# Gates and branch projections with the activations as the stationary operand

## The chip, the cores and the metric

The kernel runs on one core of a Trainium2 chip. The metric is the device time of one execution in microseconds; lower is better. Every matmul is preceded by the load of its stationary operand (PEld in the profile); the other operand moves through the array column by column.

## What is computed

A decoder trunk of two layers on 256 tokens of width 1024, in float32. The attention heads are 12 of dilated windows (branch a), 6 of block attention (b) and 6 of stick-breaking attention (c). The part around the change:

```python
h = rmsnorm(x, norm_mix)
proj = h @ w_in                                   # q, k, v and three gates of width 1024
gates = jax.nn.sigmoid(proj[..., 3 * MIX_WIDTH:]).reshape(B, S, 3, D)
y_a = flat(o_a) @ w_out_a                         # 256 -> 1024
y_b = flat(o_b) @ w_out_b                         # 384 -> 1024
y_c = flat(o_c) @ w_out_c                         # 384 -> 1024
merged = gates[:, :, 0] * y_a + gates[:, :, 1] * y_b + gates[:, :, 2] * y_c
x = x + merged @ w_o
h = rmsnorm(x, norm_mlp)
x = x + jnp.square(jax.nn.relu(h @ w_up)) @ w_down
```

## The kernel before

The activations lie transposed: channels on the 128 partitions in 8 tiles (KT), the 256 tokens (S) along the free dimension. For precision each float32 operand is split into a high and a low part of a shorter format (hi, lo), and each product is three matmuls: hi by lo of the weight, hi by hi, lo by hi.

**Weights** come in 280 pieces of 128 x 1024 (140 a layer), in the order in which they are used. load (L91) fetches a piece by DMA into one of 4 raw buffers; split_one (L106) makes its parts, wh by ScalarE (L115) and wl by VectorE (L116), in 6 buffers each, three pieces ahead of use and at raised priority. proj (L188) multiplies one weight tile, stationary, with the activations of all 256 tokens, moving: 3 matmuls of 256 columns for each of the 8 channel tiles, 24 in all.

**Stages of a layer**: values (v_chunk, L232, with activations stationary and 512 weight columns moving); queries and keys (qk_pair, L261) and gates (gate_tile, L453), between which units of the attention (att_softmax, att_c) are put as MIX_ORDER (L50) and UNIT_RATE (L44) say; the sigmoids; the **branch stage** (L489 to L503); the output projection (L506 to L513); then the MLP (up_pair, L539; down, L554, and in the last layer down_nat, L581, which has activations stationary).

gate_tile(d) makes the three gates of one channel tile, 3 x 24 matmuls into two PSUM banks, which ScalarE copies to G[d] (L459). After the last exponential of the layer, ScalarE loads the table of the sigmoid, applies it to G[0] to G[7] (L483) and, in the first layer, loads the table of exp and ln back (L486). The branch stage goes by channel tile d: into one s tile of two PSUM banks come the three branch projections (2, 3 and 3 channel tiles of oT), VectorE multiplies all 768 columns by the gates (L499), adds the three parts (L500, L501), and ScalarE and VectorE split the sum into mg (L502, L503). The output projection then takes mg as its moving operand, and VectorE adds the result to the residual xres (L511), from which norm_split (L152) makes the operand of the MLP.

**PSUM** has 8 banks: two of tag mm, two of tag t, and two s tiles of two banks each. **The order** on each engine is made by a scheduler ahead of time from the order in the program, the priorities and its own estimates; the engines then run their lists strictly in that order and wait on semaphores.

Of the kernel before, what the change touches and what calls it, by code (L numbers as in the profile page):

```python
# [15 lines left out]
P = 128  # L16
# [24 lines left out]
NORM_ACT = False  # L41
TAIL = 4
SKEW = 2
UNIT_RATE = {"v": 2, "qk": 1, "g": 2}  # L44
SWAP = [8, 9, 10, 11, 12, 13, 14, 15, 0, 1, 2, 3, 4, 5, 6, 7] + list(range(16, 32))

# [12 lines left out]
def trunk(ctx: ExitStack, tc: tile.TileContext, w, x, norms, gfin, consts, out):  # L59
# [18 lines left out]
    def mm_bank():  # L78
        return PS("mm", [P, 512], 2)
# [67 lines left out]
    negtri, negones = tri[:, 0], tri[:, 1]  # L147

    def hilo_slot():
        return T("hl", [P, 2, KT, S], 2, F32R)  # L150

    def norm_split(hl, nrm, d):  # L152

        g = cst["norms"][:, nrm, d:d + 1]
        act.activation(hl[:, 0, d], xres[:, d], AF.Copy, scale=g)
        dve.scalar_tensor_tensor(hl[:, 1, d], xres[:, d], g, hl[:, 0, d].bitcast(F32),
                                 op0=ALU.mult, op1=ALU.subtract)

    def sumsq(d, acc):
# [28 lines left out]
    def proj(dst, n, hl, nk=KT, first=True, last=True, koff=0, woff=0):  # L188

        hi, lo = split(n)  # L190
        for k in range(nk):
            c = (woff + k) * P
            a = (first and k == 0)
            z = (last and k == nk - 1)
            pe.matmul(dst, lo[:, c:c + P], hl[:, 0, koff + k], start=a, stop=False, skip_group_check=True)  # L195
            pe.matmul(dst, hi[:, c:c + P], hl[:, 0, koff + k], start=False, stop=False, skip_group_check=True)  # L196
            pe.matmul(dst, hi[:, c:c + P], hl[:, 1, koff + k], start=False, stop=z, skip_group_check=True)  # L197

    acc = T("acc", [P, S], 1)
    hl = hilo_slot()  # L200
# [9 lines left out]
    for layer in range(DEPTH):  # L210
# [9 lines left out]
        def normalized():  # L220

            for d in range(KT):
                t = T("sq", [P, S], 3)
                g = cst["norms"][:, 2 * layer, d:d + 1]
                dve.scalar_tensor_tensor(t, xres[:, d], g, R, op0=ALU.mult, op1=ALU.mult)
                act.activation(xh[:, 0, d], t, AF.Copy)
                dve.tensor_tensor(xh[:, 1, d], t, xh[:, 0, d].bitcast(F32), op=ALU.subtract)  # L227


        V = {}  # L230
# [1 line left out]
        def v_chunk(c, n):  # L232
            if c == 0:
                pv = [mm_bank(), mm_bank()]
            else:
                sb = s_bank()
                pv = [sb[:, 0], sb[:, 1]]
            for q in range(4):
                hi, lo = split(n + q)
                for kk in range(2):  # L240
                    k = 2 * q + kk
                    wsl = slice(kk * 512, kk * 512 + 512)
                    for t in range(2):
                        tsl = slice(t * P, t * P + P)
                        pe.matmul(pv[t], xs[:, 0, k, tsl], lo[:, wsl], start=k == 0, stop=False)  # L245
                        pe.matmul(pv[t], xs[:, 0, k, tsl], hi[:, wsl], start=False, stop=False)
                        pe.matmul(pv[t], xs[:, 1, k, tsl], hi[:, wsl], start=False, stop=k == KT - 1)  # L247
# [46 lines left out]
            dve.tensor_tensor(oF[j * DH:(j + 1) * DH], po[0:DH, 0:S], tmp, op=ALU.add)  # L294

        def o_split(oF, kt):
            last_exp[0] = act.activation(oT[:, 0, kt], oF, AF.Copy)
            dve.tensor_tensor(oT[:, 1, kt], oF, oT[:, 0, kt].bitcast(F32), op=ALU.subtract)

        def pv_mm(po, head, kt, ph, pl, first, last):  # L300

# [158 lines left out]

        units = []

# [4 lines left out]

        n = base
        for kind, i in MIX_ORDER:
            {"v": v_chunk, "qk": qk_pair, "g": gate_tile}[kind](i, n)  # L470
            n += MIX_LEN[kind]
            group, u = ATT_AFTER.get((kind, i), (None, 0))
            if group == "a":
                att_softmax(QK_A[u], u, units)
            elif group == "b":
                att_softmax([QK_B[u]], 2 + u, units)
            elif group == "c":
                att_c(u, units)
            run_units(UNIT_RATE[kind])
        run_units(len(units))  # L480
        with tc.issue_after(last_exp[0].ins):
            for d in range(KT):
                s = act.activation(G[d], G[d], AF.Sigmoid)  # L483
# [6 lines left out]
        for d in range(KT):  # L490
# [12 lines left out]
            dve.tensor_tensor(mg[:, 1, d], m3[:, 0], mg[:, 0, d].bitcast(F32), op=ALU.subtract)  # L503


        acc = T("acc", [P, S], 1)  # L506
        hl = hilo_slot()
        for d in range(KT):
            p = mm_bank() if d % 2 else t_bank()
            proj(p[:, 0:S], base + 68 + d, mg)  # L510
# [28 lines left out]
        def up_pair(i):  # L539
            p = mm_bank()  # L540
            proj(p[:, 0:S], npc["u", 2 * i], hl)
            proj(p[:, S:2 * S], npc["u", 2 * i + 1], hl)
            s1 = T("wk", [P, 512], WK)
            act.activation(s1, p, AF.Relu)
            u = T("wk", [P, 512], WK)
            act.activation(u, s1, AF.Square)
            uh = T("ga", [P, 2, S], KT, F32R)
            ul = T("ga", [P, 2, S], KT, F32R)
# [131 lines left out]
def weight_pieces(w_in, w_out_a, w_out_b, w_out_c, w_o, w_up, w_down):  # L680
    out = np.empty((DEPTH * PIECES, P, 1024), np.float32)

    def cols(w, f):
        return w[:, f * P:(f + 1) * P].reshape(KT, P, P).transpose(1, 0, 2).reshape(P, 1024)

    for layer in range(DEPTH):
        n = layer * PIECES
        wi = w_in[layer]
# [6 lines left out]
        for kind, i in MIX_ORDER:  # L695
            if kind == "v":
                out[n:n + 4] = vcols(i)
            elif kind == "qk":
                out[n] = cols(wi[:, :MIX], i)
                out[n + 1] = cols(wi[:, MIX:2 * MIX], i)  # L700
            else:
                for b in range(3):
                    out[n + b] = cols(gw[:, b * D:(b + 1) * D], i)
            n += MIX_LEN[kind]
        wy = np.concatenate([w_out_a[layer], w_out_b[layer], w_out_c[layer]], axis=0)
        for d in range(KT):
            out[n] = cols(wy, d)
            n += 1
        for d in range(KT):
            out[n] = cols(w_o[layer], d)  # L710
            n += 1
# [37 lines left out]
```

## Time and profile before

| | us |
|---|---|
| median of 3 runs (lowest, highest) | 893.87 (893.34, 893.88) |
| the profiled execution | 893.46 |
| its span in the profile | 891.4 |
| busy: TensorE matmul / weight load | 878.8 / 837.8 |
| busy: VectorE / ScalarE / GpSimd | 602.4 / 491.7 / 52.4 |

The difference of 2.06 us between the profiled execution and its span lies outside the profile's first and last instruction. A matmul's record is longer than its step, because matmuls overlap in the array: what counts is the distance of the starts.

### The profile page before, as it was taken

To read this page: it belongs to the slowest core of one execution; us is meant where nothing else is said; L and a number is where in the kernel's file an instruction comes from. 1 tells how busy PE (TensorE), PEld (TensorE's weight loads), DVE (VectorE), ACT (ScalarE), POOL (GpSimd) and SP (SyncE) were. 2 spreads that over 40 slices of the span, in tenths; PEclk is the share of its full clock that TensorE was granted. 3 is DMA by queue.
4 is the path that set the end of the run, shared out by engine and by line. 5 is a ranking of instruction groups with operands and counts; after the bars stand their busy time and mean duration, and the time that the engine had idled before them with its cause. 6 is when DMAs were issued, how large, how long until landed. Compare 5 with 4: busy or idle time off the path is not lost.

```text
span 891.4 us, 16382 instructions
## 1 busy us (share of the span) xinstructions
PE 878.8 (99%) x6672; PEld 837.8 (94%) x6672; DVE 602.4 (68%) x899; ACT 491.7 (55%) x724; POOL 52.4 (6%) x72
## 2 busy tenths in 40 slices
PE   8999999999999999999999999999999999999996
PEld 6899999999999999999988999999999999999995
DVE  7887787774985455555588878777667865555554
ACT  5655566668465444444466555666573654444442
POOL 6000000000020000000020100000000400000000
PEclk9999999999999999999999999999999999999999
DMA  8764444544656656555556544444555666666641
GB/s 302 232 197 144 140 129 138 158 147 131 199 167 192 193 183 189 182 177 185 165 176 203 167 148 136 141 125 139 164 165 168 194 197 192 186 186 189 187 137 47
DMA packets 43562, 151.47 MB, mean 170 GB/s; under 512 B 4960, under 2 KB 6368, under 8 KB 43488
## 3 DMA queue, kind: packets, MB, share of 16 engines
q1 hardware_dynamic: 43056, 149.90, 54.6%
q8 instruction: 52, 0.85, 0.4%
q10 hardware_dynamic: 432, 0.54, 0.2%
q14 instruction: 22, 0.18, 0.1%
HBM read 149.37 MB, written 1.05 MB: 169 GB/s over the span
## 4 chain that ended last, share of the span: by engine, by line
PE 94%; DVE 3%; issue 1%; DMA 1%; ACT 0%; SPq 0%; POOLq 0%; DVEq 0%; ACTq 0%
PE mm L195 18%; PE mm L197 18%; PE mm L196 18%; PE s L561 3%; PE s L563 3%; PE s L562 3%; PE s L587 3%; PE s L588 3%; PE s L589 3%; PE s L280 2%; PE s L195 2%; PE s L197 2%; PE s L196 2%; PE s L245 2%; DVE wl L116 2%; PE s L247 2%
## 5 line engine op out<-in xcount | busy, mean ns | idle before, releaser
L116 DVE TENSOR_TENSOR wl<-raw,wh 128x1024 fp32r<-128x1024 f32 (+1 forms) x282 | 345.5, 1228 | 228.2 <-ACT wh L115 227.4
L115 ACT ACTIVATE wh<-raw 128x1024 fp32r<-128x1024 f32 (+1 forms) x282 | 295.2, 1051 | 296.4 <-PE mm L197 160.8
L195 PE MATMUL mm<-hl,wl 128*128 128x256 f32 x1344 | 383.2, 285 | 1.4 <-DVE xres L511 1.4
L196 PE MATMUL mm<-hl,wh 128*128 128x256 f32 x1344 | 381.5, 284 | 0.0
L197 PE MATMUL mm<-hl,wh 128*128 128x256 f32 x1344 | 380.1, 284 | 0.0
L195 PEld LDWEIGHTS mm<-hl,wl 128*128 128x128 f32 x1344 | 257.1, 191 | 5.8 <-DVE xres L511 1.8
L196 PEld LDWEIGHTS mm<-hl,wh 128*128 128x128 f32 x1344 | 257.1, 191 | 0.9
L197 PEld LDWEIGHTS mm<-hl,wh 128*128 128x128 f32 x1344 | 256.5, 191 | 0.7 <-DVE hl L227 0.2
L561 PE MATMUL s<-ga,wl 128*128 128x256 f32 x256 | 72.5, 284 | 0.0
L562 PE MATMUL s<-ga,wh 128*128 128x256 f32 x256 | 72.3, 283 | 0.0
L563 PE MATMUL s<-ga,wh 128*128 128x256 f32 x256 | 72.2, 283 | 0.0
L587 PE MATMUL s<-wl,ga 128*128 128x512 f32 x128 | 50.1, 391 | 0.0
L588 PE MATMUL s<-wh,ga 128*128 128x512 f32 x128 | 50.0, 391 | 0.0
L561 PEld LDWEIGHTS s<-ga,wl 128*128 128x128 f32 x256 | 49.1, 192 | 0.5 <-DVE sq L648 0.2
L589 PE MATMUL s<-wh,ga 128*128 128x512 f32 x128 | 49.5, 389 | 0.0
L562 PEld LDWEIGHTS s<-ga,wh 128*128 128x128 f32 x256 | 49.1, 192 | 0.1
L563 PEld LDWEIGHTS s<-ga,wh 128*128 128x128 f32 x256 | 49.0, 192 | 0.2 <-DVE ga L550 0.2
L166 POOL TENSOR_TENSOR acc<-acc,sq 128x256 f32<-128x256 f32 x21 | 20.8, 991 | 404.4 <-ACT sq L165 229.8
L195 PE MATMUL s<-hl,wl 128*128 128x256 f32 x128 | 36.4, 285 | 0.0
L197 PE MATMUL s<-hl,wh 128*128 128x256 f32 x128 | 36.3, 284 | 0.0
L196 PE MATMUL s<-hl,wh 128*128 128x256 f32 x128 | 36.2, 283 | 0.0
L587 PEld LDWEIGHTS s<-wl,ga 128*128 128x128 f32 x128 | 24.1, 188 | 5.0 <-DVE V L622 0.4
(139 smaller groups left out, 1143.4 us busy)
## 6 DMA issues: line engine op xcount, KB each, us to landing
raw<-in_w_dram SPq DMA_DIRECT2D x278, 512.0 KB, 4.0
raw<-in_w_dram SPq DMA_DIRECT2D x4, 256.0 KB, 4.7
xres<-in_x_dram SPq DMA_DIRECT2D x8, 128.0 KB, 5.1
wk<-in_gfin_dram SPq DMA_DIRECT2D x2, 256.0 KB, 4.0
out_dram<-V SPq DMA_DIRECT2D x2, 256.0 KB, 2.3
out_dram<-V ACTq DMA_DIRECT2D x2, 256.0 KB, 2.2
c_maskA<-in_maskA_dram SPq DMA_DIRECT2D x1, 384.0 KB, 5.4
c_rope<-in_rope_dram SPq DMA_DIRECT2D x1, 256.0 KB, 4.9
```

Source lines behind the costliest of these rows:

```text
L115: act.activation(hi[:, c:c + step], r[:, c:c + step], AF.Copy)
L116: dve.tensor_tensor(lo[:, c:c + step], r[:, c:c + step], hi[:, c:c + step].bitcast(F32), op=ALU.subtract)
L166: pool.tensor_tensor(acc, acc, sq, op=ALU.add)
L195: pe.matmul(dst, lo[:, c:c + P], hl[:, 0, koff + k], start=a, stop=False, skip_group_check=True)
L196: pe.matmul(dst, hi[:, c:c + P], hl[:, 0, koff + k], start=False, stop=False, skip_group_check=True)
L197: pe.matmul(dst, hi[:, c:c + P], hl[:, 1, koff + k], start=False, stop=z, skip_group_check=True)
L561: pe.matmul(dst, lo[:, c], uh[:, j % 2], start=a, stop=False, skip_group_check=True)
L562: pe.matmul(dst, hi[:, c], uh[:, j % 2], start=False, stop=False, skip_group_check=True)
L563: pe.matmul(dst, hi[:, c], ul[:, j % 2], start=False, stop=z, skip_group_check=True)
L587: pe.matmul(dst, uh[:, j % 2, k], lo[:, c], start=j == 0, stop=False)
L588: pe.matmul(dst, uh[:, j % 2, k], hi[:, c], start=False, stop=False)
L589: pe.matmul(dst, ul[:, j % 2, k], hi[:, c], start=False, stop=j == 2 * npairs - 1)
```

## The change

Gates and branch projections are computed with tokens on the partitions: the activations of 128 tokens are the stationary operand, and 512 weight columns move. gate_chunk (L455 of the changed kernel) makes 512 columns of one gate for both token halves t in the two mm banks, in two halves of the contraction, with a unit of attention between them; there are 6 chunks of 4 pieces a layer for 8 tiles of 3. The branch stage (L504 to L531) goes by column half h, branch br and token half t: an s tile has one bank for each t, VectorE multiplies it by the gate (L519, L522) and adds it to the sum m[t] (L523). As the output projection wants channels on partitions, TensorE transposes m[t] in four 128 x 128 blocks into a t bank (L527), and ScalarE and VectorE split from there into mg (L530, L531). The first two tiles of the output projection are computed in two halves of the contraction (L537 to L539). In the activation tiles hi and lo now lie next to each other for each channel tile (layout [P, KT, 2, S] for [P, 2, KT, S]). The gates lie in 6 buffers of 4 KB a partition for 8 of 3 KB; the up stage of the MLP puts uh and ul in one such buffer, six pairs for four. The core of the diff:

```diff
-             ("g", 5), ("g", 6), ("g", 7)]
-MIX_LEN = {"v": 4, "qk": 2, "g": 3}
+             ("g", 5)]
+MIX_LEN = {"v": 4, "qk": 2, "g": 4}
+BRANCH_K = [(0, 1), (2, 3, 4), (5, 6, 7)]
...
-        G = [T("ga", [P, 3, S], KT) for _ in range(KT)]
-
-        def gate_tile(d, n):
-            gf = G[d].rearrange("p a b -> p (a b)")
-            for b0, nb in ((0, 2), (2, 1)):
-                p = mm_bank()
-                for b in range(nb):
-                    proj(p[:, b * S:(b + 1) * S], n + b0 + b, xh)
-                act.activation(gf[:, b0 * S:(b0 + nb) * S], p[:, 0:nb * S], AF.Copy)
+        G = {}
+
+        def gate_chunk(i, n):
+
+            G[i] = T("ga", [P, 2, 512], GA_BUFS)
+            pg = [mm_bank(), mm_bank()]
+            for half in range(2):
+                for t in range(2):
+                    tsl = slice(t * P, t * P + P)
+                    for q in (2 * half, 2 * half + 1):
+                        hi, lo = split(n + q)
+                        for kk in range(2):
+                            k = 2 * q + kk
+                            wsl = slice(kk * 512, kk * 512 + 512)
+                            pe.matmul(pg[t], xh[:, k, 0, tsl], lo[:, wsl], start=k == 0, stop=False)
+                            pe.matmul(pg[t], xh[:, k, 0, tsl], hi[:, wsl], start=False, stop=False)
+                            pe.matmul(pg[t], xh[:, k, 1, tsl], hi[:, wsl], start=False, stop=k == KT - 1)
+                    if half == 1:
+                        act.activation(G[i][:, t], pg[t], AF.Copy)
+                if half == 0:
+                    run_units(1)
...
-        for d in range(KT):
-            n = base + 60 + d
-            st = s_bank()
-            sf = st.rearrange("p a b -> p (a b)")
-            proj(sf[:, 0:S], n, oT, nk=2, koff=0, woff=0)
-            proj(sf[:, S:2 * S], n, oT, nk=3, koff=2, woff=2)
-            proj(sf[:, 2 * S:3 * S], n, oT, nk=3, koff=5, woff=5)
-            m3 = T("wk", [P, 3, S], WK)
-            m3f = m3.rearrange("p a b -> p (a b)")
-            dve.tensor_tensor(m3f, sf[:, 0:3 * S], G[d].rearrange("p a b -> p (a b)"), op=ALU.mult)
-            dve.tensor_tensor(m3[:, 0], m3[:, 0], m3[:, 1], op=ALU.add)
-            dve.tensor_tensor(m3[:, 0], m3[:, 0], m3[:, 2], op=ALU.add)
-            act.activation(mg[:, 0, d], m3[:, 0], AF.Copy)
-            dve.tensor_tensor(mg[:, 1, d], m3[:, 0], mg[:, 0, d].bitcast(F32), op=ALU.subtract)
+        for h in range(2):
+            n = base + 60 + 4 * h
+            m = [T("wk", [P, 512], WK) for t in range(2)]
+            for br, ks in enumerate(BRANCH_K):
+                st = s_bank()
+                for t in range(2):
+                    tsl = slice(t * P, t * P + P)
+                    for k in ks:
+                        hi, lo = split(n + k // 2)
+                        wsl = slice(k % 2 * 512, k % 2 * 512 + 512)
+                        pe.matmul(st[:, t], oT[:, k, 0, tsl], lo[:, wsl], start=k == ks[0], stop=False)
+                        pe.matmul(st[:, t], oT[:, k, 0, tsl], hi[:, wsl], start=False, stop=False)
+                        pe.matmul(st[:, t], oT[:, k, 1, tsl], hi[:, wsl], start=False, stop=k == ks[-1])
+                    g = G[2 * br + h][:, t]
+                    if br == 0:
+                        dve.tensor_tensor(m[t], st[:, t], g, op=ALU.mult)
+                    else:
+                        y = T("wk", [P, 512], WK)
+                        dve.tensor_tensor(y, st[:, t], g, op=ALU.mult)
+                        dve.tensor_tensor(m[t], m[t], y, op=ALU.add)
+            for t in range(2):
+                tb = t_bank()
+                for d in range(4):
+                    pe.transpose(tb[:, d * P:(d + 1) * P], m[t][:, d * P:(d + 1) * P], ident)
+                t4 = tb.rearrange("p (a b) -> p a b", a=4)
+                mh, ml = (mg[:, 4 * h:4 * h + 4, x, t * P:(t + 1) * P] for x in range(2))
+                act.activation(mh, t4, AF.Copy)
+                dve.tensor_tensor(ml, t4, mh.bitcast(F32), op=ALU.subtract)
...
+        pw = [mm_bank(), mm_bank()]
+        for first in (True, False):
+            for d in range(2):
+                proj(pw[d][:, 0:S], base + 68 + d, mg, nk=4, first=first, last=not first, koff=0 if first else 4, woff=0 if first else 4)
```

**The order at three places** of the first layer, as the programs have it; in brackets stand the engines on whose semaphores an instruction waits. First TensorE in the branch stage before: s_465, s_470 and s_475 are the s tiles of three channel tiles, and 24 matmuls stand between one mark and the next.

```order
L195 MATMUL s_465_2668<-hl_23_169,wl_454_2561 128x256
L196 MATMUL s_465_2668<-hl_23_169,wh_453_2560 128x256
L197 MATMUL s_465_2668<-hl_23_169,wh_453_2560 128x256
...
L195 MATMUL s_470_2705<-hl_23_169,wl_458_2593 128x256 [waits DVE_49]
L196 MATMUL s_470_2705<-hl_23_169,wh_457_2592 128x256
L197 MATMUL s_470_2705<-hl_23_169,wh_457_2592 128x256
...
L195 MATMUL s_475_2742<-hl_23_169,wl_463_2635 128x256 [waits DVE_49]
```

The same place now: s_456 is the tile of branch a (6 matmuls for each token half), s_460 that of b, s_469 that of c (9 each), which takes the buffer of s_456; all of column half 0. Runs of matmuls between the marks are left out.

```order
L516 MATMUL s_456_2333<-wh_445_2263,hl_23_169 128x512
...
L514 MATMUL s_460_2354<-wl_452_2300,hl_23_169 128x512 [waits Activation_49]
...
L516 MATMUL s_460_2354<-wh_451_2299,hl_23_169 128x512 [waits DVE_49]
L514 MATMUL s_456_2333<-wl_446_2264,hl_23_169 128x512 [waits DVE_49]
L515 MATMUL s_456_2333<-wh_445_2263,hl_23_169 128x512
...
L514 MATMUL s_469_2391<-wl_452_2300,hl_23_169 128x512 [waits DVE_49]
L515 MATMUL s_469_2391<-wh_451_2299,hl_23_169 128x512
...
L514 MATMUL s_460_2354<-wl_449_2288,hl_23_169 128x512 [waits DVE_49]
```

The second token half of s_456 waits for VectorE after 9 other matmuls, and s_469 waits for VectorE directly behind it. Second, ScalarE at the sigmoids before; ga_24 to ga_31 are the gates of the eight channel tiles.

```order
L297 ACTIVATE hl_23_169<-oF_356_2002 128x256 [waits DVE_49]
L483 ACT_TABLE_LOAD
L483 ACTIVATE ga_24_170<-ga_24_170 128x768
...
L483 ACTIVATE ga_29_175<-ga_29_175 128x768 [waits Activation_49]
L483 ACTIVATE ga_30_176<-ga_30_176 128x768 [waits Activation_49]
...
L459 ACTIVATE ga_31_177<-mm_448_2527 128x512
...
L459 ACTIVATE ga_31_177<-mm_455_2589 128x256
...
L483 ACTIVATE ga_31_177<-ga_31_177 128x768 [waits Activation_49]
L486 ACT_TABLE_LOAD
```

The same place now.

```order
L299 ACTIVATE hl_23_169<-oF_376_1992 128x256 [waits DVE_49]
L497 ACT_TABLE_LOAD
L497 ACTIVATE ga_135_793<-ga_135_793 128x1024
L497 ACTIVATE ga_235_1316<-ga_235_1316 128x1024
L497 ACTIVATE ga_331_1783<-ga_331_1783 128x1024
L497 ACTIVATE ga_382_2009<-ga_382_2009 128x1024
L497 ACTIVATE ga_418_2151<-ga_418_2151 128x1024 [waits Activation_49]
L497 ACTIVATE ga_438_2246<-ga_438_2246 128x1024 [waits Activation_49]
L500 ACT_TABLE_LOAD
L117 ACTIVATE wh_471_2397<-raw_470_2395 128x1024 [waits DMAHW2_49,PE_49]
```

Before, gate evictions still followed on the first seven sigmoids; now all of them stand ahead of the sigmoids, and the next weight split stands behind the six sigmoids and the load of the table. Third, VectorE at the end of the branch stage now; wk_478 is the sum of column half 1 and token half 1, t_498 the transposes of token half 0. Before there were no transposes, and this place had only the products, sums and splits of the channel tiles.

```order
L118 TENSOR_TENSOR wl_509_2566<-raw_507_2563,wh_508_2565 128x1024 [waits DMAHW0_49,Activation_49]
L522 TENSOR_TENSOR wk_497_2524<-s_492_2496,ga_438_2246 128x512 [waits PE_49]
L118 TENSOR_TENSOR wl_514_2619<-raw_512_2616,wh_513_2618 128x1024 [waits DMAHW1_49,Activation_49]
L531 TENSOR_TENSOR hl_453_2330<-t_498_2527,hl_453_2330 128x4x128 [waits Activation_49]
L523 TENSOR_TENSOR wk_478_2437<-wk_478_2437,wk_497_2524 128x512 [waits DVE_49]
L531 TENSOR_TENSOR hl_453_2330<-t_499_2534,hl_453_2330 128x4x128 [waits Activation_49]
```

The last sum (L523) stands behind two weight splits and a subtraction, and the last group of transposes (t_499) needs it.

## Rows read from the trace of the kernel before

**Rows 1.** Part 1 of the page: busy us (share of the span) x instructions.

```profile
PE 878.8 (99%) x6672; PEld 837.8 (94%) x6672; DVE 602.4 (68%) x899; ACT 491.7 (55%) x724; POOL 52.4 (6%) x72
```

**Rows 2.** Part 4 of the page: the chain that ended last, by engine.

```profile
PE 94%; DVE 3%; issue 1%; DMA 1%; ACT 0%; SPq 0%; POOLq 0%; DVEq 0%; ACTq 0%
```

**Rows 3.** Timeline, TensorE, last gates of layer one: start, us, engine, line, operation.

```profile
207.76 0.28 PE L195 MATMUL mm<-hl,wl 128*128 128x256 f32 x1
...
216.28 0.28 PE L197 MATMUL mm<-hl,wh 128*128 128x256 f32 x1
```

**Rows 4.** Timeline, TensorE, down projection of the last layer, activations stationary.

```profile
741.68 0.39 PE L588 MATMUL s<-wh,ga 128*128 128x512 f32 x1
...
743.95 0.39 PE L589 MATMUL s<-wh,ga 128*128 128x512 f32 x1
```

**Rows 5.** Windows, branch stage: stretch, length, busy PE, PEld, DVE, ACT, POOL, clock, DMA.

```profile
229.00:246.00 17.00, 17.00 (x144) 17.00 (x143) 15.95 (x28) 6.91 (x11) 0.00 (x0) 1.00 0.58 162
```

**Rows 6.** Timeline, TensorE: a value matmul, three stalls, the last matmul.

```profile
207.06 0.22 PE L307 MATMUL t<-pl,V 128*64 128x128 f32 x1
...
224.08 0.28 PE L197 MATMUL s<-hl,wh 128*128 128x256 f32 x1
224.35 0.39 PE L195 MATMUL s<-hl,wl 128*128 128x256 f32 x1
...
250.25 0.28 PE L197 MATMUL mm<-hl,wh 128*128 128x256 f32 x1
250.69 0.39 PE L195 MATMUL t<-hl,wl 128*128 128x256 f32 x1 [0.16 <-DVE xres L511]
...
264.81 0.29 PE L196 MATMUL mm<-hl,wh 128*128 128x256 f32 x1
265.93 0.39 PE L195 MATMUL mm<-hl,wl 128*128 128x256 f32 x1 [0.84 <-DVE xres L511]
...
884.27 0.39 PE L589 MATMUL s<-wh,ga 128*128 128x512 f32 x1
```

**Rows 7.** Timeline, TensorE, four transposes inside a stream of matmuls.

```profile
711.13 0.60 PE L576 MATMUL t<-c_ident,xres 128*128 128x128 f32 x4
711.49 0.36 PE L197 MATMUL mm<-hl,wh 128*128 128x256 f32 x1
711.69 0.28 PE L195 MATMUL mm<-hl,wl 128*128 128x256 f32 x1
```

**Rows 8.** Groups by line and form: count, busy us, mean ns, idle before.

```profile
L116 DVE TENSOR_TENSOR wl<-raw,wh 128x1024 fp32r<-128x1024 f32 x278 | 341.5, 1231 | 222.5 <-ACT wh L115 221.7
L115 ACT ACTIVATE wh<-raw 128x1024 fp32r<-128x1024 f32 x278 | 292.7, 1057 | 292.1 <-PE mm L197 160.8 <-PE s L563 38.9 <-PE s L589 33.7
L272 DVE TENSOR_TENSOR qk<-qk,sh 128x512 f32<-128x512 f32 x18 | 12.4, 686 | 0.2
L483 ACT ACTIVATE ga<-ga 128x768 f32<-128x768 f32 x16 | 12.2, 832 | 0.0
L270 DVE TENSOR_TENSOR qk<-mm,c_rope 128x512 f32<-128x512 f32 x18 | 12.1, 672 | 0.0
L459 ACT ACTIVATE ga<-mm 128x512 f32<-128x512 f32 x16 | 9.4, 589 | 0.1
```

**Rows 9.** Timeline, ScalarE, around the sigmoids of the first layer.

```profile
209.64 0.42 ACT L297 ACTIVATE hl<-oF 128x256 fp32r<-128x256 f32 x1 [1.06 <-DVE oF L294]
210.08 1.28 ACT L483 ACT_TABLE_LOAD   x1
211.37 5.25 ACT L483 ACTIVATE ga<-ga 128x768 f32<-128x768 f32 x7
...
222.05 1.28 ACT L486 ACT_TABLE_LOAD   x1
```

**Rows 10.** Windows at the end of the trace, same columns as rows 5.

```profile
888.00:889.00 1.00, 0.00 (x0) 0.00 (x0) 0.00 (x0) 0.00 (x0) 0.00 (x0) 0.60 0.45 170
889.00:890.00 1.00, 0.00 (x0) 0.00 (x0) 0.00 (x0) 0.00 (x0) 0.00 (x0) 0.50 0.91 354
```

More of the change, by code (lines that the diff above doesn't have):

```diff
@@ L43 @@
 SKEW = 2
+GA_BUFS = 6
 UNIT_RATE = {"v": 2, "qk": 1, "g": 2}
@@ L149, in hilo_slot @@
     def hilo_slot():
-        return T("hl", [P, 2, KT, S], 2, F32R)
+        return T("hl", [P, KT, 2, S], 2, F32R)
     def norm_split(hl, nrm, d):
         g = cst["norms"][:, nrm, d:d + 1]
-        act.activation(hl[:, 0, d], xres[:, d], AF.Copy, scale=g)
-        dve.scalar_tensor_tensor(hl[:, 1, d], xres[:, d], g, hl[:, 0, d].bitcast(F32),
+        act.activation(hl[:, d, 0], xres[:, d], AF.Copy, scale=g)
+        dve.scalar_tensor_tensor(hl[:, d, 1], xres[:, d], g, hl[:, d, 0].bitcast(F32),
                                  op0=ALU.mult, op1=ALU.subtract)
@@ L194, in proj @@
             z = (last and k == nk - 1)
-            pe.matmul(dst, lo[:, c:c + P], hl[:, 0, koff + k], start=a, stop=False, skip_group_check=True)
-            pe.matmul(dst, hi[:, c:c + P], hl[:, 0, koff + k], start=False, stop=False, skip_group_check=True)
-            pe.matmul(dst, hi[:, c:c + P], hl[:, 1, koff + k], start=False, stop=z, skip_group_check=True)
+            pe.matmul(dst, lo[:, c:c + P], hl[:, koff + k, 0], start=a, stop=False, skip_group_check=True)
+            pe.matmul(dst, hi[:, c:c + P], hl[:, koff + k, 0], start=False, stop=False, skip_group_check=True)
+            pe.matmul(dst, hi[:, c:c + P], hl[:, koff + k, 1], start=False, stop=z, skip_group_check=True)
     acc = T("acc", [P, S], 1)
@@ L225, in normalized @@
                 dve.scalar_tensor_tensor(t, xres[:, d], g, R, op0=ALU.mult, op1=ALU.mult)
-                act.activation(xh[:, 0, d], t, AF.Copy)
-                dve.tensor_tensor(xh[:, 1, d], t, xh[:, 0, d].bitcast(F32), op=ALU.subtract)
+                act.activation(xh[:, d, 0], t, AF.Copy)
+                dve.tensor_tensor(xh[:, d, 1], t, xh[:, d, 0].bitcast(F32), op=ALU.subtract)
         V = {}
@@ L244, in v_chunk @@
                         tsl = slice(t * P, t * P + P)
-                        pe.matmul(pv[t], xs[:, 0, k, tsl], lo[:, wsl], start=k == 0, stop=False)
-                        pe.matmul(pv[t], xs[:, 0, k, tsl], hi[:, wsl], start=False, stop=False)
-                        pe.matmul(pv[t], xs[:, 1, k, tsl], hi[:, wsl], start=False, stop=k == KT - 1)
+                        pe.matmul(pv[t], xs[:, k, 0, tsl], lo[:, wsl], start=k == 0, stop=False)
+                        pe.matmul(pv[t], xs[:, k, 0, tsl], hi[:, wsl], start=False, stop=False)
+                        pe.matmul(pv[t], xs[:, k, 1, tsl], hi[:, wsl], start=False, stop=k == KT - 1)
             V[c] = T("V", [P, 2, 8, 2, DH], 3, F32R)
@@ L296, in o_split @@
         def o_split(oF, kt):
-            last_exp[0] = act.activation(oT[:, 0, kt], oF, AF.Copy)
-            dve.tensor_tensor(oT[:, 1, kt], oF, oT[:, 0, kt].bitcast(F32), op=ALU.subtract)
+            last_exp[0] = act.activation(oT[:, kt, 0], oF, AF.Copy)
+            dve.tensor_tensor(oT[:, kt, 1], oF, oT[:, kt, 0].bitcast(F32), op=ALU.subtract)
         def pv_mm(po, head, kt, ph, pl, first, last):
@@ L481, in trunk @@
         with tc.issue_after(last_exp[0].ins):
-            for d in range(KT):
-                s = act.activation(G[d], G[d], AF.Sigmoid)
+            for i in range(6):
+                s = act.activation(G[i], G[i], AF.Sigmoid)
         if layer < DEPTH - 1:
@@ L506, in trunk @@
         acc = T("acc", [P, S], 1)
         hl = hilo_slot()
+        pw = [mm_bank(), mm_bank()]
+        for first in (True, False):
+            for d in range(2):
+                proj(pw[d][:, 0:S], base + 68 + d, mg, nk=4, first=first, last=not first, koff=0 if first else 4, woff=0 if first else 4)
         for d in range(KT):
-            p = mm_bank() if d % 2 else t_bank()
-            proj(p[:, 0:S], base + 68 + d, mg)
+            if d < 2:
+                p = pw[d]
+            else:
+                p = mm_bank() if d % 2 else t_bank()
+                proj(p[:, 0:S], base + 68 + d, mg)
@@ L546, in up_pair @@
             act.activation(u, s1, AF.Square)
-            uh = T("ga", [P, 2, S], KT, F32R)
-            ul = T("ga", [P, 2, S], KT, F32R)
+            uu = T("ga", [P, 2, 2, S], GA_BUFS, F32R)
+            uh, ul = uu[:, 0], uu[:, 1]
             dve.tensor_copy(uh.rearrange("p a b -> p (a b)"), u)
@@ L684, in cols, with halves @@
         return w[:, f * P:(f + 1) * P].reshape(KT, P, P).transpose(1, 0, 2).reshape(P, 1024)
+    def halves(w):
+        return w.reshape(KT // 2, 2, P, 512).transpose(0, 2, 1, 3).reshape(4, P, 1024)
     for layer in range(DEPTH):
@@ L701, in weight_pieces @@
             else:
-                for b in range(3):
-                    out[n + b] = cols(gw[:, b * D:(b + 1) * D], i)
+                out[n:n + 4] = halves(gw[:, i * 512:(i + 1) * 512])
             n += MIX_LEN[kind]
         wy = np.concatenate([w_out_a[layer], w_out_b[layer], w_out_c[layer]], axis=0)
-        for d in range(KT):
-            out[n] = cols(wy, d)
-            n += 1
+        for h in range(2):
+            out[n:n + 4] = halves(wy[:, h * 512:(h + 1) * 512])
+            n += 4
         for d in range(KT):
```

3 lines of the change are left out of this document (1 added, 2 removed).

## The prediction

> **What bounds the kernel now.** I read the page's busy shares first: TensorE is busy for 99% of the span [rows 1]. As matmuls are pipelined, that proves little, so the chain of waits comes next: 94% of it is TensorE, 3% VectorE [rows 2]. The kernel is bound by the rate at which matmuls follow each other, and that is read from the start times in the timeline. Matmuls with 256 moving columns start 0.120 us apart, 72 of them without a gap from 207.76 to 216.28 [rows 3]. With 512 columns it is 0.227 us, ten steps from 741.68 to 743.95 [rows 4]. One wide matmul thus replaces two narrow ones and saves 0.240 - 0.227 = 0.013 us. VectorE is the second thing to watch: in the branch stage it is busy 15.95 of 17 us [rows 5] while TensorE does not wait for it. TensorE loses almost nothing there now: three stalls in each layer, of 0.15, 0.32 and 1.0 us beyond the step of 0.12 [rows 6].
>
> **The change, part by part.**
> *Gates.* Before, 8 tiles x 3 x 24 = 576 narrow matmuls per layer; now 6 chunks x 48 = 288 wide ones. *Branch projections.* 8 x 24 = 192 narrow ones become 2 x 8 x 2 x 3 = 96 wide ones. Together 384 per layer, 768 in all, x 0.013 = **-10.0 us**, all on the bounding engine.
>
> The Trainium skill (TensorE: Matmul & The Clock Gate, "Back-to-back issue gap") speaks against this gain: N/2.4 + 2.5 ns gives 109 ns and 216 ns for the two widths, a saving of 2.6 ns, so 2.0 us in all and a time of 914. The rows have 120 and 227 ns in long unbroken stretches, and I go by them.
>
> *Transposes.* 4 groups of 4 per layer are new. Four such transposes stand inside a stream of narrow matmuls: from 711.13 to 711.49, and the step after them is 0.08 too long, so 0.44 us a group [rows 7]. 8 groups: **+3.5 us**.
>
> *The branch stage's waits.* This is where I expect the loss. Before, one s tile took three projections (24 matmuls, 2.9 us) and two such tiles alternated, so VectorE had 2.9 us to empty one. Now a tile holds two token halves, and its second half waits for VectorE to have multiplied the first; the next use of the tile waits for the multiply of the second. The order shows these waits on TensorE, with little or nothing between a half and the matmul that waits for its reading. Prices, all from [rows 8] unless named: a multiply out of PSUM 0.67, an add or a subtraction 0.69, a weight split 1.06 on ScalarE and then 1.23 on VectorE (an operation that is followed at once counts 0.07 less), the copy out of PSUM 0.59; a wide matmul's result is there 0.39 after its start [rows 4], 0.16 after the next could start. I add about 0.04 for each hand-over. First layer:
> 1. The first multiply needs the first sigmoid, which follows the last head's split. Before, that split ended at 210.06 [rows 9], 3.0 us after the last value matmul at 207.06 [rows 6]; the table load took 1.28 [rows 9]. A sigmoid of 1024 columns is estimated at 0.83 + 0.24 = 1.07 (768 columns take 0.83, a 512-column eviction 0.59). So 3.0 + 1.28 + 1.07 + 0.67 + 0.1 = 6.1 us until TensorE may write the second half. It has 14 wide matmuls before that, 3.2 us: **2.9**. Before, gate matmuls filled this time: the table load began at 210.08, the gates ended at 216.28 [rows 3, 9].
> 2. The tile's next use directly behind its second half: 0.16 + 0.67 + 0.1 = **0.9**.
> 3. The second tile's next use waits for a multiply that stands on VectorE behind a weight split, and this stands on ScalarE behind all six sigmoids and the table load back: from the first sigmoid's start 5.9 + 1.28 + 1.06 + 1.16 + 0.67 = 10.1 us (six sigmoids, each overlapping the last by 0.1 as the seven in 5.25 us do now [rows 9]). TensorE gets there after the first sigmoid and multiply (1.8), 6 wide matmuls (1.36), step 2 (0.9) and 18 more (4.08), together 8.1: **2.0**. The second layer has no table load back; there step 2's 0.9 binds.
> 4. The next: a split waits for a weight buffer that TensorE frees, then 1.06 + 1.16 + 0.67 + 0.1 = 3.0, against 1.6 of matmuls and transposes: **1.4**.
> 5. The next: 0.9 less the 0.44 of a transpose group between: **0.5**.
> 6. The last transpose group needs the last sum. VectorE has before it, in its order, a split that waits for ScalarE, the multiply, another split, a subtraction, and then the add: 1.06 + 1.16 + 0.65 + 1.16 + 0.62 + 0.69 + 0.1 = 5.4 us from the moment the weight buffer is freed; TensorE has 5 wide matmuls and 4 transposes, 1.6: **3.9**.
>
> Sum 11.6 in the first layer, 10.5 in the second: **+22.1 us**. Bounds from both sides: if TensorE never waits, 0; if each of the 12 (tile, half) pairs of a layer waited for its own multiply, 12 x 0.9 = 11 and step 6 on top, 15 a layer.
>
> *The old stalls.* Two of the three were waits for adds to the residual that VectorE was late with [rows 6]. After step 6's pause VectorE has caught up, so I take all three as gone: 2 x 1.47 = **-2.9** (bound: 0).
>
> *At nothing.* ScalarE evicts the same gate columns in 24 pieces of 512 [rows 8]; as many weight pieces are loaded and split. VectorE has 24 operations of 512 columns per layer in the branch stage, 16.4 us. The new order of hi and lo in the activation tiles only moves addresses. The up stage has six pairs of buffers for four. TensorE waits for none of these now, being 94% of the chain [rows 2]; if VectorE's 16.4 us did reach the path, that is what the six steps price.
>
> Sum: -10.0 + 3.5 + 22.1 - 2.9 = **+12.7**. The profiled execution took 893.46 (span 891.4 and 2.06 around it), 0.41 under the median; with the median, 893.87 + 12.7 = 906.6. I say **906**.
>
> **Rivals.**
> *A, the waits are covered (faster).* The two halves lie in separate banks, and a queue that runs ahead could read one while the other is written. Then only -10.0 + 3.5 remain: 887. It decides at 4.7 us of new stalls a layer ((10.0 - 3.5 + 2.9) / 2). For it: TensorE waits almost nowhere now. Against: VectorE at 15.95 of 17 us has no room, and the order has the waits. Chance 0.07.
> *B, VectorE's queue is less late than I reckon.* Splits come earlier, so steps 3 and 4 fall to 0.9 and 0.5, and step 6 to the multiply, the add and a subtraction less the transposes, 1.8. Then 2.9 + 0.9 + 0.9 + 0.5 + 0.5 + 1.8 = 7.5 a layer, 15 in all: 893.9 - 10.0 + 3.5 + 15 - 2.9 = 899.5. Chance 0.17.
> *C, the pause costs clock.* At the end of the trace the granted clock falls from 1.00 to half (2.4 to 1.2 GHz) at about 888.2, 0.60 in 888 to 889 and 0.50 after it [rows 10], when TensorE had started its last matmul at 884.27 [rows 6]. Step 6 leaves it idle for nearly 4 us after several shorter stalls. Each microsecond at half speed costs 0.5; no row shows how long it would last. Between 0 and the whole output projection of some 20 us (10 a layer) I take 2 a layer: 910. Chance 0.15. The same page of the Trainium skill ("Why this matters for your kernels") warns of exactly such idle gaps between bursts of matmuls; the end of the trace agrees.
> *D, the wide matmuls gain little* in these stages (2 of the 10.0, say): 914. Against it, both stretches of wide matmuls run at 0.227. Chance 0.03.
>
> **How the numbers follow.** The forecast has 0.58, with a range of its own of 903 to 909. The range of 8 in 10 takes in B and C: 898 to 911; it leaves out A, D and the edges of B and C. A measurement here can tell 0.2%, 1.8 us. Faster by that: A, 0.07. Within it: 0.02, from between A and B. Slower: 0.91.
>
> **What would show it.** Right: in the timeline, wide matmuls 0.227 apart in the gates; transposes 0.11 apart; TensorE idle before the projections' first and second halves, the releaser VectorE's multiply or ScalarE's sigmoid, 10 to 12 us a layer; the longest idle time, near 4 us, before the last group of transposes; VectorE idle before weight splits that wait for ScalarE in the branch stage. Wrong: an idle time under 5 us in the branch stage (A), or a granted clock under 1.00 after the pause (C), or wide matmuls more than 0.23 apart (D).

## The result and the profile after

The changed kernel takes **919.29 us** (median of 4 runs, 918.31 to 920.57) against 893.88 (4 runs): ratio 1.0288, 95% interval 1.0276 to 1.0301. The direction was right, the size was not: 906 was forecast, 898 to 911 the range. The profiled execution took 918.96 (span 917.2), 25.5 more than the one before. Part 1 of the page, against [rows 1]:

```profile
PE 887.9 (97%) x5936; PEld 800.9 (87%) x5936; DVE 601.6 (66%) x883; ACT 492.6 (54%) x704; POOL 58.0 (6%) x72
```

TensorE has 736 matmuls less and is busy 9 us longer, in a span that is 26 us longer. So waits and dearer matmuls both have to be looked for. First the waits, TensorE's by releaser (us in total, times, longest):

```profile
PE t L527 <- DVE wk L523: 7.2, 2, 3.6
PE s L514 <- DVE wk L519: 6.5, 6, 2.1
PE s L514 <- DVE wk L522: 4.6, 4, 1.4
...
PE s L514 <- ACT hl L299: 1.0, 2, 0.5
```

They sum to 19.3, all in the branch stage. In the timeline of the first layer they stand where the six steps put them:

```profile
217.74 0.39 PE L516 MATMUL s<-wh,hl 128*128 128x512 f32 x1
218.65 0.50 PE L514 MATMUL s<-wl,hl 128*128 128x512 f32 x1 [0.52 <-ACT hl L299]
218.99 0.40 PE L515 MATMUL s<-wh,hl 128*128 128x512 f32 x1
221.74 0.51 PE L514 MATMUL s<-wl,hl 128*128 128x512 f32 x1 [2.12 <-DVE wk L519]
224.19 0.51 PE L514 MATMUL s<-wl,hl 128*128 128x512 f32 x1 [0.78 <-DVE wk L519]
229.99 0.50 PE L514 MATMUL s<-wl,hl 128*128 128x512 f32 x1 [1.44 <-DVE wk L522]
233.53 0.60 PE L527 MATMUL t<-c_ident,wk 128*128 128x128 f32 x4
235.34 0.51 PE L514 MATMUL s<-wl,hl 128*128 128x512 f32 x1 [1.21 <-DVE wk L522]
239.86 0.50 PE L514 MATMUL s<-wl,hl 128*128 128x512 f32 x1 [0.35 <-DVE wk L519]
...
253.24 0.63 PE L527 MATMUL t<-c_ident,wk 128*128 128x128 f32 x4 [3.62 <-DVE wk L523]
253.62 0.36 PE L197 MATMUL t<-hl,wl 128*128 128x256 f32 x1
253.82 0.28 PE L198 MATMUL t<-hl,wh 128*128 128x256 f32 x1
```

Steps 1 to 6 were forecast at 2.9, 0.9, 2.0, 1.4, 0.5 and 3.9; they are 0.52 + 2.12, 0.78, 1.44, 1.21, 0.35 and 3.62: 10.04. In the second layer they are 9.38.

A stall costs more than this idle time, which is counted from the end of a record. A wide matmul's record is 0.39 long, but the next matmul could have started after 0.23; so the first stall, with 0.91 between the starts at 217.74 and 218.65, costs 0.68 and not 0.52. Behind a group of transposes (record 0.60, next start after 0.38) a stall costs 0.22 more than its idle time. The forecast counted from where the next matmul could start. Counted so, the steps of the first layer are 2.96, 0.95, 1.60, 1.43, 0.57 and 3.84, together 11.4 for 11.6 forecast, and those of the second layer 10.7 for 10.5: **22.1** for 22.1. On top comes the first step behind a stall, 0.34 instead of 0.23 (218.65 to 218.99), after 12 of the 14 stalls: 1.4 in all.

The last rows price a group of transposes: 0.38 from its start to the next matmul, and 0.08 too long a step behind it, 0.46 (in [rows 7] 0.44).

The pace of the wide matmuls in the last gate chunk, 18 steps without a gap:

```profile
209.76 0.39 PE L468 MATMUL mm<-wh,hl 128*128 128x512 f32 x1
...
213.87 0.39 PE L468 MATMUL mm<-wh,hl 128*128 128x512 f32 x1
```

That is 4.11 / 18 = 0.2283, so a wide matmul saves 0.0117 against the two narrow ones of [rows 3], and 768 save 9.0.

Three more things were not in the sum. **The scores** (query times key, 64 rows of the array for each head), by form: before, then after:

```profile
L280 PE MATMUL s<-qk 64*128 64x256 f32 x72 | 11.6, 405 | 0.0
L280 PE MATMUL s<-qk 64*128 64x128 f32 x72 | 8.1, 297 | 0.0
L284 PE MATMUL s<-qk 64*128 64x128 f32 x24 | 4.2, 288 | 0.0
L284 PE MATMUL s<-qk 64*128 64x256 f32 x24 | 4.2, 428 | 0.0
```

```profile
L282 PE MATMUL s<-qk 64*128 64x256 f32 x72 | 17.7, 411 | 0.0
L282 PE MATMUL s<-qk 64*128 64x128 f32 x72 | 8.1, 297 | 0.0
L286 PE MATMUL s<-qk 64*128 64x256 f32 x24 | 4.2, 428 | 0.0
L286 PE MATMUL s<-qk 64*128 64x128 f32 x24 | 2.7, 305 | 0.0
```

The count and the duration of one are nearly the same; the busy time, in which records of one form that overlap count once, goes from 28.1 to 32.7. From the start of each run of scores to the next other matmul it is 24.0 and 28.8 (12.0 and 14.4 a layer): +4.8. The change doesn't touch these lines, but its unit in the middle of a gate chunk cuts their runs: 30 runs before, 38 after. Twelve records of 256 columns, in one run before, and in runs of four, two and six after:

```profile
123.77 1.57 PE L280 MATMUL s<-qk 64*128 64x256 f32 x12
125.26 0.38 PE L195 MATMUL mm<-hl,wl 128*128 128x256 f32 x1
```

```profile
118.67 1.13 PE L282 MATMUL s<-qk 64*128 64x256 f32 x4
119.73 0.39 PE L308 MATMUL t<-ph,V 128*128 128x256 f32 x1
...
124.98 0.40 PE L469 MATMUL mm<-wh,hl 128*128 128x512 f32 x1
125.31 0.70 PE L282 MATMUL s<-qk 64*128 64x256 f32 x2
125.93 0.50 PE L469 MATMUL mm<-wh,hl 128*128 128x512 f32 x1
126.27 0.40 PE L467 MATMUL mm<-wl,hl 128*128 128x512 f32 x1
...
129.29 1.56 PE L282 MATMUL s<-qk 64*128 64x256 f32 x6
130.78 0.49 PE L469 MATMUL mm<-wh,hl 128*128 128x512 f32 x1
```

The one run takes 1.49, the three take 1.06 + 0.62 + 1.49 = 3.17: six records by themselves take as long as twelve. In the run of twelve the records start in pairs, 0.007 apart, and the next pair follows after 0.216; in the cut runs single records follow each other after 0.216. (The layer's earlier run of twelve, only in part in pairs, took 2.03 and is 3.17 now, too.) The code computes the two heads of a pair in turn; that a cut run holds one head alone is my reading, since the trace doesn't name the head. The steps ahead of a run and behind it are 0.1 too long on either side (124.98 to 125.31 and 125.93 to 126.27, 0.33 and 0.34 for 0.23), so a run more costs 0.2. The Trainium skill (TensorEngine Tiling (Array Packing), "Key Properties") says that different tiles of the array can work in parallel and that a change of the tiling mode drains the engine; the pairs and the borders here agree with both.

**The clock**, in windows of the second layer (length, busy TensorE with its matmuls, granted clock, DMA):

```profile
670.00:672.00 2.00, 1.24 (x4) 0.81 0.16 66
672.00:678.00 6.00, 5.22 (x13) 0.50 0.04 7
...
704.00:706.00 2.00, 1.66 (x12) 0.85 0.73 269
706.00:708.00 2.00, 2.00 (x12) 0.50 0.35 141
```

It fell twice to half (2.4 to 1.2 GHz): first behind the stalls of 0.52 and 2.12, then behind the pause of 3.62. In the first layer it stayed at 1.00 through the same stalls and the same pause, so the difference of the layers prices it. From the end of the first stall to the first transposes: 14.88 with 4.34 of waits in the first layer (218.65 to 233.53), 17.00 with 3.68 in the second, so +2.1 and the 0.66 that it waited less: +2.8. The 60 records behind the last transposes take 7.66 (253.24 to 260.90) and 9.14 (704.34 to 713.48), so +1.5. Together 4.3.

**The place of the hidden layer's pairs** in memory is told at e10_before_gates_late.

### The profile page after: what moved, and what is told of

Its sections match the earlier page's. It is cut to its first block, busy times and chain, and to the rows that moved or that the text cites. A ratio compares the mean times of both kernels' runs of the same rounds, so it can differ in the third digit from the quotient of the medians.

```text
span 917.2 us, 14875 instructions
## 1 busy us (share of the span) xinstructions
PE 887.9 (97%) x5936; PEld 800.9 (87%) x5936; DVE 601.6 (66%) x883; ACT 492.6 (54%) x704; POOL 58.0 (6%) x72
## 4 chain that ended last, share of the span: by engine, by line
PE 93%; DVE 2%; ACT 2%; DMA 1%; issue 1%; SPq 0%; POOLq 0%; ACTq 0%; DVEq 0%
PE mm L197 13%; PE mm L199 13%; PE mm L198 13%; PE mm L467 5%; PE mm L469 5%; PE mm L468 5%; PE s L596 3%; PE s L598 3%; PE s L597 3%; PE s L622 3%; PE s L624 3%; PE s L623 3%; PE s L282 2%; PE s L247 2%; PE s L249 2%; PE s L248 2%
## 5 line engine op out<-in xcount | busy, mean ns | idle before, releaser
L197 PE MATMUL mm<-hl,wl 128*128 128x256 f32 x976 | 277.0, 285 | 0.0
L198 PE MATMUL mm<-hl,wh 128*128 128x256 f32 x976 | 276.8, 284 | 0.0
L199 PE MATMUL mm<-hl,wh 128*128 128x256 f32 x976 | 276.2, 285 | 0.0
L197 PEld LDWEIGHTS mm<-hl,wl 128*128 128x128 f32 x976 | 186.9, 192 | 2.2 <-ACT wh L117 0.7
L198 PEld LDWEIGHTS mm<-hl,wh 128*128 128x128 f32 x976 | 187.0, 192 | 0.9
L199 PEld LDWEIGHTS mm<-hl,wh 128*128 128x128 f32 x976 | 186.3, 192 | 0.3
L467 PE MATMUL mm<-wl,hl 128*128 128x512 f32 x192 | 77.0, 401 | 0.0
L469 PE MATMUL mm<-wh,hl 128*128 128x512 f32 x192 | 76.0, 396 | 0.0
L468 PE MATMUL mm<-wh,hl 128*128 128x512 f32 x192 | 75.9, 395 | 0.0
L168 POOL TENSOR_TENSOR acc<-acc,sq 128x256 f32<-128x256 f32 x21 | 20.1, 956 | 411.1 <-ACT sq L167 237.9
L467 PEld LDWEIGHTS mm<-wl,hl 128*128 128x128 f32 x192 | 36.1, 188 | 8.5 <-issue 1.3
```

What stands on the lines that cost most here:

```text
L197: pe.matmul(dst, lo[:, c:c + P], hl[:, koff + k, 0], start=a, stop=False, skip_group_check=True)
L198: pe.matmul(dst, hi[:, c:c + P], hl[:, koff + k, 0], start=False, stop=False, skip_group_check=True)
L199: pe.matmul(dst, hi[:, c:c + P], hl[:, koff + k, 1], start=False, stop=z, skip_group_check=True)
L467: pe.matmul(pg[t], xh[:, k, 0, tsl], lo[:, wsl], start=k == 0, stop=False)
L468: pe.matmul(pg[t], xh[:, k, 0, tsl], hi[:, wsl], start=False, stop=False)
L469: pe.matmul(pg[t], xh[:, k, 1, tsl], hi[:, wsl], start=False, stop=k == KT - 1)
```

## The experiments

Theory 1: the waits come from the shared s tile and VectorE's order. Theory 2: the unit in the middle of a gate chunk makes the scores dearer. Theory 3: the place of tiles in the on-chip memory changes the pace of the down projections. The median of the kernel before, measured beside each, was 893.45 to 893.70. Behind a run's time stand its ratio to that and the 95% interval. A busy time or a wait is of the profiled execution.

### e1_gates_only and e2_branch_only

The new gates with the branch stage and output projection of before, and the reverse.

```diff
-            for br, ks in enumerate(BRANCH_K):
...
+            proj(sf[:, 0:S], n, oT, nk=2, koff=0, woff=0)
```

> The gates of the change with the branch stage of before (gates are then read in the wrong layout, so the output is not the reference's; the count of operations in the branch stage is that of before). 576 narrow matmuls become 288 wide ones, 576 x 0.013 = -7.5 us: 886.4 if that is all the new gates do. Theory 2 (the attention units now stand in the middle of a gate chunk too, so that score matmuls of the two heads of a pair no longer alternate): the score matmuls take 14.4 us a layer instead of 12.0, so +4.8 and 891.2. If gates and branch stage shared the loss in another way (wide gate matmuls dear), 895 or more.

> The branch stage of the change with the gates of before (gates are read in the wrong layout). Theory 1 (the loss is in the waits for the shared s tile and VectorE's order): pace 192 x 0.013 = -2.5, transposes +3.5, old stalls -2.9; of the 22 us of waits step 1 (2.9 a layer) is covered by gate matmuls again and step 3 falls to 0.9, so about 15: 907, and up to 5 more if the clock falls after the last pause as it did in the second layer of the change. Score matmuls at 12.0 us a layer. Rival (the loss is the gates' or needs both parts): 896 or less.

Measured: e1 **897.27** (1.0043, 1.0029 to 1.0058), e2 **908.12** (1.0159, 1.0142 to 1.0176). The gates alone lose, with the scores at 28.8 from start to start (14.4 a layer) as Theory 2 expects, but 6 us more than it gave. Of the 6, 0.8 are the pace (576 x 0.0117 is 6.7, not 7.5), 0.7 the pairs' place (e10), about 1.6 the borders of 8 runs more at 0.2. The rest fits stalls at the head of the branch stage that the kernel before has not:

```profile
PE s L197 <- DVE wk L513: 0.9, 3, 0.4
PE s L197 <- ACT hl L299: 0.6, 2, 0.3
```

They are 1.5 of idle time, 2.3 from start to start, 2.8 with the first steps behind them. e2 is as Theory 1 has it, and its rival falls. Its waits:

```profile
PE t L515 <- DVE wk L511: 7.2, 2, 3.6
PE s L502 <- DVE wk L510: 4.0, 4, 1.2
```

With 0.7 more they are 11.9, or 13.5 from start to start. Here the clock fell behind the pause in both layers:

```profile
248.00:250.00 2.00, 0.57 (x3) 0.50 0.77 240
```

The 60 records behind it take 10.03 (249.43 to 259.46) and 9.14 where 7.66 is full speed: 3.9. So 893.45 - 192 x 0.0117 + 3.2 (transposes) - 2.7 (old stalls) + 13.5 + 0.7 (first steps) + 3.9 = 909.8; the profiled execution took 909.98. It is the longest of the four (906.50 to 909.98), and its mean granted clock, 0.994, the lowest (0.997 in the shortest).

The losses of e1 and e2, 3.8 and 14.7, add up to 18.5 of the change's 25.4. Most of what needs both parts is in the waits, 11.9 in e2 and 19.3 in the change.

### e3_two_tiles

```diff
-                st = s_bank()
+                st = [s_bank()[:, 0], mm_bank()]
```

> The change, with a PSUM tile of its own for each token half of a branch (the second half in one of the banks of the gates), so that no matmul waits for the multiply of the other half. Theory 1 (sharing of the tile): steps 2 to 5 go and step 6 becomes short, some 14 us less, and with the pause the fall of the clock (about 5): 900; 905 if the clock falls all the same. Rival (VectorE has no room in that stage, whatever the tiles): the waits move to the next use of a tile or to the transposes, 914 or more.

Measured: **899.21** (1.0065, 1.0050 to 1.0080). Theory 1 holds, its rival falls. VectorE does the same work, and of the waits in the branch stage and the output projection 5.3 are left, 1.5 of them in three smaller groups:

```profile
PE mm L197 <- DVE wk L522: 2.9, 2, 1.5
...
PE s L514 <- DVE wk L519: 0.9, 2, 0.5
```

The granted clock stays at 1.00 through both branch stages. From start to start and with the first steps, the stalls cost 23.5 in the change and 7.4 here; these 16.1 and 4.3 of clock are 20.4, and 20.1 were won.

### e4_no_mid_units, e5_two_tiles_no_mid and e6_gates_only_no_mid

```diff
-                if half == 0:
-                    run_units(1)
```

The two lines go: in e4 from the change, in e5 from e3, in e6 from e1; in e5 and e6 three units follow each chunk instead of two.

> The change without the attention unit in the middle of a gate chunk (units run only between chunks). Theory 2: the score matmuls come back to 12.0 us a layer, 4.8 us less: 914.5, if the branch stage's waits stay as they are. Rival (the scores are longer because of the new order of hi and lo in the activation tiles or of the wide matmuls before them): scores stay at 14.4 a layer, 919.

> The change with a tile of its own for each half (as in e3_two_tiles), without the unit in the middle of a gate chunk, and with three units instead of two after each chunk, so that the attention does not end later. Theory 2 (the order of the units costs the scores 2.4 us a layer, and it stays won where the branch stage does not wait for late attention): 899.2 - 4.8 = 894.4, up to 2 less as there are fewer switches between kinds of matmuls; scores at 12.0 us a layer, no stretch at half clock. Rival (what the scores gain is given back by the end of the attention, as in e4_no_mid_units): scores at 12.0, but 897 to 900, with waits of TensorE for the exponentials and for the first sigmoid.

> The gates of the change with the branch stage of before (gates read in the wrong layout), without the unit in the middle of a gate chunk and with three units after each. Theory 2: 897.3 - 4.8 = 892.5, so that new gates alone gain a little over before. Rival (the gates' loss is in wide matmuls at 0.229 and in switches, not in the scores' order): 896 or more with scores at 14.4.

Measured: e4 **920.45** (1.0303, 1.0288 to 1.0319), e5 **897.69** (1.0045, 1.0028 to 1.0061), e6 **891.68** (0.9980, 0.9971 to 0.9989). The scores' busy time falls as Theory 2 says, in e4 from 32.7 to 27.5 (28 runs; 23.9 from start to start), most of it in the form that had grown, and e4's rival falls:

```profile
L282 PE MATMUL s<-qk 64*128 64x256 f32 x72 | 13.6, 405 | 0.0
```

In e6 it is 29.4 (32 runs; three units a chunk cut others), 3.3 less than in e1, and the time is 5.6 less: of the 2.3 over, 6 runs fewer at 0.2 make 1.2 and two stalls fewer at the head of the branch stage 1.0. The new gates alone are then 0.2% faster than before. But in e4 nothing is left of the 5.2. The attention ends later, and TensorE waits for that:

```profile
PE s L512 <- ACT hl L299: 2.9, 2, 1.4
...
PE t L308 <- ACT ph L385: 1.5, 2, 0.7
```

And the clock now falls in the first layer too, where the change kept it; over both layers 27 us pass at half clock, 10 in the change:

```profile
220.00:228.00 8.00, 6.25 (x14) 0.50 0.01 2
```

In e5, with two tiles, half is given back: 3.3 of scores less, 1.5 won, and the time is the rival's (897 to 900), not my 894. TensorE waits 2.9 for the first products (e3: 0.9) but not for exponentials. That the gates no longer cover the sigmoids is my reading; no run singled it out.

### e7_pairs_apart, e8_pairs_moved and e10_before_gates_late

Why did the down projections change their pace? The kernel before, by line, the first layer's (256 columns) and the second's (512), with the mean ns of one at the end; in the change they are 282 and 396:

```profile
L561 PE MATMUL s<-ga,wl 128*128 128x256 f32 x256 | 72.5, 284 | 0.0
...
L587 PE MATMUL s<-wl,ga 128*128 128x512 f32 x128 | 50.1, 391 | 0.0
```

e7 takes one tile for each part of a pair again, e8 other slots and distances:

```diff
-            uu = T("ga", [P, 2, 2, S], GA_BUFS, F32R)
+            uh = T("ga", [P, 2, S], GA_BUFS, F32R)
+            ul = T("ga", [P, 2, S], GA_BUFS, F32R)
```

> As e3_two_tiles, with the two parts of the squared hidden layer in a tile each (as before the change) in slots of 4 KB, three pairs instead of six. Open question: why the down projections of the first layer went from 0.1200 to 0.1184 us a narrow matmul and those of the second from 0.228 to 0.2332 a wide one. If it is the merging into one tile (one wait for both parts), the steps return to 0.1200 and 0.228, and the time to 899.2 + 1.3 - 2.0 = 898.5. If it is where the tiles lie (multiples of 4 KB now, of 3 KB before), the steps stay at 0.1184 and 0.2332: 899.2, and more if three pairs are too few.

> As e5_two_tiles_no_mid, with gates in four tiles of 6 KB (one for each output half and token half, all three branches in it; four sigmoids of 1536 columns for six of 1024), and the pairs of the hidden layer in the same slots: in the first layer the second part 2 KB behind the first, in the second layer 3 KB, as before the change. If the place of the parts sets the pace of the down projections: second layer back from 0.2332 to 0.228 (-2.0), first layer at 0.1184 if the distance of 2 KB is what counts, at 0.1200 if slots of 4 KB are: 895.7 or 897. If neither counts: 897.7 as e5, with steps of 0.1184 and 0.2332.

Measured: e7 **899.25** (1.0063, 1.0048 to 1.0078), e8 **898.67** (1.0059, 1.0043 to 1.0076); both at 282 and 396 ns, as the change. Neither merging, nor slots, nor distance: both readings of mine fell. (e8 is 1.0 slower than e5; its wait for the first products is 3.7 for 2.9.) What was left is that the program gives each group of tiles its place at its first use, and the change uses the gates' group first in a gate chunk and no longer at the start of the layer. e10 makes that move in the kernel before, and no other:

```diff
-        G = [T("ga", [P, 3, S], KT) for _ in range(KT)]
+        G = {}
...
+            G[d] = T("ga", [P, 3, S], KT)
```

> The kernel before, with the eight gate tiles created one by one where each is first used instead of all at the start of the layer. The order of the instructions stays; the storage of the gates and of the hidden pairs moves behind the other tiles of the on-chip memory, as the change moved it, and the weights' tiles move down by 24 KB. Theory 3 (the place of these tiles alone changed the pace in the down projections): first layer 768 narrow steps from 0.1200 to 0.1184 (-1.2), second layer 384 wide ones from 0.228 to 0.2332 (+2.0): 893.9 + 0.8 = 894.5. Rival (it is another part of the change): steps stay at 0.1200 and 0.228, time 893.7.

Measured: **894.29** (1.0006, 0.9997 to 1.0015), and in e10's trace:

```profile
L562 PE MATMUL s<-ga,wl 128*128 128x256 f32 x256 | 72.1, 282 | 0.0
...
L588 PE MATMUL s<-wl,ga 128*128 128x512 f32 x128 | 50.6, 396 | 0.0
```

Theory 3 holds: the change's paces, in the kernel before, from the place alone. TensorE's order of instructions is the same as before. In the other runs the paces go with the place, too: e2, which has the change's branch stage and activation layout but makes its gate tiles at the start of the layer, shows the old ones. Narrow steps gain, wide ones lose; both together are 0.7, which the times alone could not tell from nothing (the interval takes in 1).

### e9_pool_adds and e11_best

```diff
-                        dve.tensor_tensor(m[t], m[t], y, op=ALU.add)
+                        (pool if br == 1 else dve).tensor_tensor(m[t], m[t], y, op=ALU.add)
```

> As e8_pairs_moved, with the add of the second branch's product on GpSimd instead of VectorE (4 adds of 512 columns a layer, 0.69 us each, 2.8 us a layer off VectorE). Theory 1 in its second half (with two tiles VectorE's order is what is left of the waits: 2.9 + 1.6 us of waits for its products and sums in e5): 3 to 4 us less than e8_pairs_moved, 892 to 893. Rival (the remaining waits are for weight splits and ScalarE, or GpSimd's add, slower than VectorE's, is itself late for the second add): as e8_pairs_moved or slower.

> All that helped, together: two tiles for the halves, no unit in the middle of a gate chunk and three after each, the third gate chunk behind the last pair of the query and key projections (so that no chunk cuts a run of scores and four chunks lie at the end), the second branch's add on GpSimd, and the gates and hidden pairs in two groups of three 4 KB tiles, one behind the other tiles (used by the pairs of the first layer), one before them (used by the pairs of the second). From e9_pool_adds at 896.2: scores back to 12.0 (-1.6), about 1.5 less of waits for the first products, and -2.0 if the pairs' place sets the pace of the second layer: 891, faster than before by 0.3%. If only the scores' order and the first waits count: 893. Rival (waits return at the end of the attention, as in e4_no_mid_units): 896.

Measured: e9 **896.19** (1.0027, 1.0018 to 1.0036), 2.5 less than e8 (3 to 4 were expected) though GpSimd's add takes 1.78 where VectorE's took 0.68 in the change: VectorE's order was part of the waits, which fell from 8.1 to 5.2 in the branch stage and the output projection. e11 **890.22** (0.9965, 0.9952 to 0.9979), 0.35% faster than the kernel before, with an interval that leaves out 1; its parts were not taken apart further. Its trace has the scores at 27.5 and the second layer's wide matmuls back at their old duration, with the pairs in front of the other tiles:

```profile
L619 PE MATMUL s<-wl,gb 128*128 128x512 f32 x128 | 50.1, 391 | 0.0
```

and of the branch stage's waits 4.8 instead of 19.3 (with 0.6 for the last head's split):

```profile
PE s L511 <- DVE wk L516: 2.9, 2, 1.4
...
PE t L524 <- DVE wk L520: 1.3, 2, 0.9
```

## Why the prediction was wrong

**Its own sum came out.** Pace -10.0 was -9.0; transposes +3.5 were 8 x 0.38 and 0.08 behind the two groups that no stall follows, +3.2; the six steps' +22.1 were +22.1, counted as the forecast counted them; the old stalls' -2.9 were -2.7 (in the second layer they were 0.14, 0.32 and 0.74 beyond the step) and are gone: TensorE waits nowhere for the residual. That makes +13.6 where +12.7 was said. The first step behind each stall was not priced, +1.4. By the formula of the Trainium skill (TensorE: Matmul & The Clock Gate, "Back-to-back issue gap"), which the section gives for an isolated matmul, the pace would have given 2.0; the rows give 9.0 and were the better guide.

**The step that failed is "At nothing".** It lists evictions, weight pieces, VectorE's operations, addresses and buffers, and leaves out the unit of attention that the change puts inside a gate chunk, which the section on the change and its diff both show. The unit moves score matmuls, which I took as unchanged work: +4.8 from start to start (+4.6 in busy time) and, with 8 runs more at 0.2, about +1.6 at their borders. The paragraph also takes moved addresses and buffers as free: +0.7, by e10.

**Rival C was placed wrongly, and its price is luck.** I had one fall of the clock a layer, 2 us each, as an alternative to the forecast with a chance of 0.15. It came twice in one layer and not in the other, 4.3 in all, near my 4; but 2.8 of that are the first fall, behind stalls of 0.52 and 2.12, where I had looked at the long pause alone. A rival that only adds to the forecast should have moved the top of the range: with 4 of clock on the 906 and some 6 of dearer scores the 911 was passed.

The account: 13.6 + 1.4 + 4.8 + 1.6 + 4.3 + 0.7 = 26.4, where the profiled executions differ by 25.5. Each term is good to some tenths, so nothing large is left to explain.

**Rival A** fell with 19.3 us of idle time, **B** with 3.62 at step 6, **D** with 0.2283 in the gates. Why the clock stayed up in the change's first layer is open: the same stalls stand there as ahead of both falls in the second.

## What to carry to other kernels

A halved PSUM tile is one tile for waiting: give each half its own (e3: 20 us, 4 of them clock) before counting what a faster matmul form wins. Add to a stall's idle time what the record ahead of it runs beyond its step, and the longer first step behind it. When an edit puts other work into a stretch, look at what it cuts apart: score matmuls that ran in pairs took twice as long singly. Price what would only add (a clock that falls behind a pause) into the range, not beside it.

## What I had not expected of the hardware

- Twelve score records took 1.49 us in one run, in pairs, and 3.17 in three runs; a run costs 0.1 on either side.
- The place of tiles in the on-chip memory alone moved a narrow matmul's step from 0.120 to 0.118 and a wide one's from 0.228 to 0.233 (e10; mean durations 284 to 282 and 391 to 396 ns). Whether the pairs' own place or that of the weights' tiles, which moved with it, does this is open; in e11 both moved, too. Why it does is open as well.
- The granted clock fell behind stalls of 0.5 and 2.1 us in one layer and stayed at full behind the same stalls and a pause of 3.6 in the other. In e2 and e4 it fell behind the pause in both layers. Each fall of the profiled executions lasted 3.4 to 10.2 us.
